# Hymba decoder step on one core: three prompt blocks go raw through the first projection, two of them side by side

## The chip, the core and the metric

The kernel runs on one NeuronCore of a Trainium2 chip. The metric is the device time of one execution in microseconds (us). Five engines work side by side, each with its own queue of instructions in program order: PE (TensorE, matmul), ACT (ScalarE), DVE (VectorE), POOL (GpSimd) and SP (SyncE, which in this kernel issues all DMAs before the change). "PEld" is PE's loading of stationary operands, which overlaps its matmuls.

## The reference

One layer of a decoder over 1024 prompt tokens and 32 sample tokens (8 sequences of 4), with D_MODEL 1024. Cut to what the change touches:

```python
h = rmsnorm(x, norm_w)                     # x * rsqrt(mean(x*x) + 1e-6) * norm_w, per token
proj = einsum('btd,dc->btc', h, w_in)      # 4104 columns, split among the heads
# hq, hf, hi (values of the HGRN heads), hgate | fq, fk, fv, ff, fgate
hg_v = hi                                  # 512 columns
y = x + w_out(concat[HGRN(hq, hf, hi) * silu(hgate), FoX(fq, fk, fv, ff) * silu(fgate)])
return rmsnorm(y, final_norm_w), new k, v, log-forget rows, recurrent states
```

A token's norm is one factor for the whole token. So the projection of x * norm_w without the factor, times the factor afterwards, gives the same row of values.

## The kernel before, in words

The prompt is cut into 8 blocks of 128 tokens, `tb` 0 to 7; the sample tokens are a ninth, `tb` 8 (`NB`). An input is kept as two halves of lower precision, `xhi` and `xlo`, and so is each weight (`hi`, `lo`); a product takes three matmuls (hi by hi, hi by lo, lo by hi). `Group.proj` (L357) does this for one block, for a range of the 8 slices `k` of D_MODEL, with the token block as the stationary operand and 512 weight columns streaming. A block of the first projection is 24 such matmuls into one PSUM bank; the pool `ps_pj` has two banks.

The order of every engine is the program order, written out by hand (`manual_schedule`). It has these stages:

- **Start** (L391 to L435). SP issues the loads of x (512 KB per block, `load_x`, L187) and of the weights `w_1` for the values (four pairs of slices, 512 KB each, `Group.load`). PE runs 14 matmuls on ones (`warm`, L228). Blocks 0 and 1 take a short path: ACT writes `xhi = x * norm_w` (`quick_hi`, L281), DVE writes `xlo` (`quick_lo`, L284), eight small instructions each; the token's factor comes from a square on ACT and eight one-column products on PE (`quick_sq`, `quick_r`), is kept in `rc`, and is applied by ACT when the bank is copied to `v` (L424, L435). ACT and DVE split the weights on the way (`Group.split`). PE does block 0 over all `k`, then block 1.
- **First projection** (L439 to L462), blocks 2 to 7, with the full norm. `norm_a` (L320) is a square on ACT (L243), a product with `norm_w` in place on POOL (L245) and a sum on DVE (L249). `norm_b` (L323) is one product with ones on PE, two ACT steps for the factor (L218, L219), two products on DVE (L265), two copies to `xhi` on ACT (L269) and two subtractions to `xlo` on DVE (L273). While block `tb` is on PE, `norm_b(tb + 1)` runs; `norm_a(tb + 2)` stands ahead of it. The weights `w_2` for the gates are loaded and split in between (L351, L354). ACT copies the bank to `v` at the end of a block (L462).
- **Gates** (L554 to L571). Eight groups, `gate_group` (L522), in the order tb = 2, 3, 4, 5, 6, 7, 0, 1: 48 matmuls in two halves of 260 columns, each half copied out by DVE (L526; L529 and L530). After each group comes a SiLU (`silu_mul`: ACT L379 to L381, DVE L382, ACT L383, POOL L384 and L386). Between group and SiLU stands one step of `again(0)` or `again(1)` (L298), the full norm of the two raw blocks, in three steps: the square, the POOL product and the DVE sum (L307); then the product with ones on PE, the factor, and the products (L313); then `xhi` and `xlo`. Groups 0 to 5 (by place) take one step each. Groups 3 to 5 also take a step of `lower_bound` (L511 on), groups 3 and 5 a split of the first slab (ACT L486, DVE L487).
- **The rest**: 24 slabs of 128 columns by all tokens, the HGRN recurrence, the FoX attention and the output projection, PE nearly always at work.

```python
anew = [again(0), again(1)]
for n, tb in enumerate((2, 3, 4, 5, 6, 7, 0, 1)):
    gate_group(tb)
    if n < 6:
        next(anew[n // 3])
    ...
    silu_mul(sg[tb // 2][:, tb % 2], 128)
```

Of the kernel before, what the change touches and what calls it, by code (L numbers as in the profile page):

```python
# [9 lines left out]
F32 = mybir.dt.float32  # L10
# [10 lines left out]
D = 1024  # L21
NB = 8
# [48 lines left out]
def tile_hymba(ctx, tc, x_prompt, x_sample, x_b, x_d, cache_k_t, cache_v, cache_logf_t, state_hgrn, page_table,  # L71
# [107 lines left out]
            debt[0] -= c  # L179
        debt[0] = max(debt[0], -3.0)  # L180

    A.preload_act_table_set("natural_log_exp_and_others")

    nwT = cst.tile([128, KB], F32, name="nwT")
    xts = {}

    def load_x(tb):  # L187
        n = 128 if tb < NB else ND
        xts[tb] = U((17, 18, 24, 25, 26, 27, 24, 25, 26)[tb], D, a=KB)[:, :, :n]
        SP.dma_start(xts[tb], (x_b[tb] if tb < NB else x_d).rearrange("p (k t) -> p k t", k=KB))  # L190

    cc = cst.tile([128, K_MK], F32, name="cc")
    ident = cc[:, K_ID:K_ID + 128]
# [34 lines left out]
    def warm(n):  # L228
        for _ in range(n):
            mm(pw[:, :128], ones, ones, True, True)  # L230

    warm(14)

    ss_ = {}

# [40 lines left out]

    rc = cst.tile([128, 2], F32, name="rc")

    def quick_hi(tb, k):  # L281
        A.activation(xhi[:, k, tb * 128:tb * 128 + 128], xts[tb][:, k], AF.Copy, scale=nwT[:, k:k + 1])
# [3 lines left out]
        V.scalar_tensor_tensor(xlo[:, k, t], xts[tb][:, k], nwT[:, k:k + 1], f32(xhi[:, k, t]),  # L286
                               op0=OP.mult, op1=OP.subtract)

    def quick_sq(tb):
        A.activation(U(15 + tb % 2, D, a=KB), xts[tb], AF.Square)  # L290

    def quick_r(tb):
        sq, p = U(15 + tb % 2, D, a=KB), ps_s()[:, :1]
        for k in range(KB):
            mm(p, sq[:, k], ones[:, :1], k == 0, k == KB - 1)
        rstd(rc[:, tb:tb + 1], p, D)

    def again(tb):  # L298

        xt, sq = xts[tb], U(7, D, a=KB)  # L300
        on, s, r = (U(6)[:, i * 128:i * 128 + 128] for i in range(3))
        if tb == 0:
            V.memset(on, 1.0)
        A.activation(sq, xt, AF.Square)
        for k in halves:
            G.tensor_mul(xt[:, k], xt[:, k], nwT[:, k, None].to_broadcast([128, 4, 128]))
        V.tensor_reduce(s, sq.rearrange("p k t -> p t k"), axis=AX.X, op=OP.add)  # L307
        yield
        p = ps_s()[:, :128]
        mm(p, on, s, True, True)  # L310
        rstd(r, p, D)
        for k in halves:
            V.tensor_mul(xt[:, k], xt[:, k], r[:, None, :].to_broadcast([128, 4, 128]))  # L313
        yield
        for f in (norm_hi, norm_lo):
            for k in halves:
                f(tb, k)
        yield

    def norm_a(tb):  # L320
# [67 lines left out]
    w1 = Group(w_1, range(8), (12, 13, 14, 28))  # L388
    w2 = Group(w_2, (8, 9, 10, 11, 28, 29, 4, 5), (13, 14, 12, 13))
    every = slice(0, 512)  # L390
    load_x(0)  # L391
    SP.dma_start(nwT, norm_w)
    w1.load(0)
    w1.load(1)
    load_x(1)
    w1.load(2)
    w1.load(3)
    load_x(2)
    load_x(3)
    ks = range(KB)  # L400
    for k in ks:
        quick_hi(0, k)
    for k in ks[:4]:
        quick_lo(0, k)
    w1.split(0, (V, V), (V, V))
    quick_sq(0)
    for k in ks[4:]:
        quick_lo(0, k)
    w1.split(1, (A, A), (V, V))
    load_x(4)  # L410
    load_x(5)
    SP.dma_start(cc, consts[:, :K_MK])
    pa, pb = ps_pj(), ps_pj()
    w1.proj(pa, 0, every, ks[:4])
    w1.split(2, (A, A), (V, V))
    w1.proj(pa, 0, every, ks[4:6])
    w1.split(3, (A, A), (V, V))
    quick_r(0)
    for k in ks:
        quick_hi(1, k)  # L420
    w1.proj(pa, 0, every, ks[6:])
    for k in ks:
        quick_lo(1, k)
    A.activation(v[0][:, 0], pa, AF.Copy, scale=rc[:, 0:1])  # L424
    w2.load(0)
    w2.load(1)
    red = norm_sq(2)
    quick_sq(1)
    red(0)
    w1.proj(pb, 1, every, ks)  # L430
    norm_b(2)
    quick_r(1)
    norm_a(3)
    load_x(6)
    A.activation(v[0][:, 1], pb, AF.Copy, scale=rc[:, 1:2])  # L435
    w2.load(2)
    SP.dma_start(bf, bcast_row(b_fox_f, FH))
    SP.dma_start(hw, bcast_row(hg_norm_w, HK))
    for tb in range(2, NB):  # L439
        if tb < 6:  # L440
            norm_a(tb + 2)
        if tb == 7:
            w1.proj_d(vd, every)
        ps = ps_pj()
        w1.proj(ps, tb, every, range(3))
        if tb == 6:
            norm_b(NB)
        if tb < 7:
            norm_b(tb + 1)
        if tb < 4:  # L450
            load_x(tb + 5)
        if tb == 5:
            norm_a(NB)
        w1.proj(ps, tb, every, range(3, 6))
        if tb < 5:
            w2.split(tb - 2)
        if tb == 3:
            w2.load(3)
        if tb == 7:
            w2.split(3)  # L460
        w1.proj(ps, tb, every, range(6, KB))
        A.activation(v[tb // 2][:, tb % 2], ps, AF.Copy)  # L462
# [87 lines left out]

    SP.dma_start(lb[:, 0], bass.AP(tensor=hg_lb.tensor, offset=hg_lb.offset, ap=[[1, 128], [128, NH]]))
    lbs = lower_bound()
    anew = [again(0), again(1)]
    for n, tb in enumerate((2, 3, 4, 5, 6, 7, 0, 1)):  # L554
        gate_group(tb)
        if n < 6:
            next(anew[n // 3])
        if n == NB - 1:
            log_sigmoid(lf.rearrange("p b h -> p (b h)"), zf.rearrange("p b h -> p (b h)"), 128, 64)
            V.tensor_copy(lfh, lf.rearrange("p b h -> p h b"))  # L560
            w2.proj_d(sgd[:, :260], slice(0, 260))
            w2.proj_d(sgd[:, 260:], slice(260, 520))
        if n in (3, 4, 5):
            next(lbs)
        silu_mul(sg[tb // 2][:, tb % 2], 128)
        if n == 0:
            slab_load(0)
        if n in (3, 5):
            slab_split(0, n // 5)
        if n == 5:  # L570
            slab_load(1)  # L571
# [986 lines left out]
```

## Time and profile before

| | |
|---|---|
| median of 3 runs | 778.69 us (778.48 to 779.23) |
| the profiled execution | 778.63 us, its span 776.8 us |
| mean granted TensorE clock | 0.985 |
| busy: PE, PEld, DVE, ACT, POOL | 744.2, 665.3, 466.2, 363.8, 314.5 us |
| DMA | 64.99 MB, mean 84 GB/s |

The span runs from the first to the last instruction; 1.8 us lie around it. "busy" counts an engine's own work, and two engines' busy times overlap. The granted clock of 1.00 is 2.4 GHz, 0.50 is 1.2 GHz.

### The profile page before, as it was taken

What the parts mean: (1) busy time and instruction counts of PE and PEld (TensorE: products, weight loads), DVE (VectorE), ACT (ScalarE), POOL (GpSimd) and SP (SyncE); (2) the same over time, 40 slices, a digit from 0 to 9 for tenths busy, and PEclk for the clock granted to TensorE, in tenths of its full rate; (3) what the DMA queues carried; (4) which work ended last, traced back from release to release, by engine and by line L of the source; (5) the groups of instructions that cost most, each with busy time, mean ns of one, the idle gap of its engine ahead of it and who ended that gap; (6) DMA issues with size and microseconds to landing.
All of it is one profiled execution on the core that took longest, in us unless ns stands there. A gap on an engine that the chain in (4) does not pass through costs nothing.

```text
span 776.8 us, 13010 instructions
## 1 busy us (share of the span) xinstructions
PE 744.2 (96%) x4835; PEld 665.3 (86%) x4835; DVE 466.2 (60%) x972; ACT 363.8 (47%) x853; POOL 314.5 (40%) x333
## 2 busy tenths in 40 slices
PE   8999989999999999998999999989999899999996
PEld 7778989998999999998998889979988786577886
DVE  5775454746647666267448854785478776667422
ACT  5663555434242432136547653757466521456322
POOL 0442545373371753635424553436344533232101
PEclk9999999999999999999999999999999999999999
DMA  8211000101221113003101011101111596713521
GB/s 332 97 35 40 1 19 12 60 7 55 82 83 58 55 32 109 28 31 117 51 29 57 30 57 53 57 30 55 55 57 57 182 334 207 266 62 119 202 81 55
DMA packets 27570, 64.99 MB, mean 84 GB/s; under 512 B 5395, under 2 KB 6547, under 8 KB 27507
## 3 DMA queue, kind: packets, MB, share of 16 engines
q1 hardware_dynamic: 27506, 64.16, 24.3%
q8 instruction: 38, 0.62, 0.3%
q14 instruction: 26, 0.21, 0.1%
HBM read 47.27 MB, written 16.88 MB: 83 GB/s over the span
## 4 chain that ended last, share of the span: by engine, by line
PE 74%; DVE 13%; ACT 8%; issue 3%; DMA 1%; POOL 1%; SPq 0%; DVEq 0%; ACTq 0%; POOLq 0%
PE pj L95 54%; PE ps L95 11%; PE po L95 3%; PE pt L966 2%; DVE u L897 2%; DVE u L971 2%; DVE st L936 1%; PE pt L95 1%; ACT u L970 1%; ACT u L946 1%; DMA u<-in_w_dram 1%; ACT xhi L269 1%; DVE u L832 1%; DVE u L853 1%; DVE u L998 1%
## 5 line engine op out<-in xcount | busy, mean ns | idle before, releaser
L95 PE MATMUL pj<-xhi,u 128*128 128x352 f32 x1152 | 316.1, 334 | 0.9 <-DVE u L487 0.5
L95 PEld LDWEIGHTS pj<-xhi,u 128*128 128x128 f32 x1152 | 207.6, 190 | 3.5 <-DVE u L487 0.8
L95 PE MATMUL pj<-xlo,u 128*128 128x352 f32 x576 | 187.1, 325 | 0.0
L95 PE MATMUL ps<-u,u 128*128 128x64 f32 (+6 forms) x984 | 133.3, 271 | 3.5 <-ACT u L946 2.6
L95 PEld LDWEIGHTS ps<-u,u 128*128 128x128 f32 (+2 forms) x984 | 115.6, 178 | 14.4 <-ACT u L946 4.4
L951 POOL TENSOR_SCALAR u<-u,st 128x128 f32<-128x128 f32 (+3 forms) x64 | 48.7, 761 | 154.2 <-DVE st L949 87.2
L95 PEld LDWEIGHTS pj<-xlo,u 128*128 128x128 f32 x576 | 109.7, 190 | 0.7
L95 PE MATMUL pj<-u,xhi 128*128 128x260 f32 (+1 forms) x384 | 91.9, 333 | 5.9 <-DVE u L526 3.4
L946 ACT ACTIVATE u<-ps,st 128x512 f32<-128x512 f32 (+2 forms) x96 | 55.1, 578 | 48.8 <-DVE st L939 21.4
L95 PEld LDWEIGHTS pj<-u,xhi 128*128 128x128 f32 x384 | 65.3, 195 | 14.1 <-DVE u L526 3.0
L696 POOL TENSOR_TENSOR u<-u,u 128x256 f32<-128x256 f32 (+1 forms) x56 | 41.9, 748 | 83.6 <-PE ps L95 78.1
L95 PE MATMUL pj<-h,u 128*128 128x512 f32 (+2 forms) x237 | 74.1, 384 | 0.5 <-DVE h L1087 0.5
L971 DVE TENSOR_TENSOR u<-pt,u 128x512 fp32r<-128x512 f32 (+1 forms) x80 | 48.5, 632 | 28.6 <-ACT u L970 28.0
L95 PE MATMUL pj<-u,xlo 128*128 128x260 f32 (+1 forms) x192 | 63.7, 332 | 0.0
L970 ACT ACTIVATE u<-pt 128x512 fp32r<-128x512 f32 (+1 forms) x80 | 41.9, 553 | 41.4 <-PE pt L966 33.8
L936 DVE TENSOR_REDUCE st<-ps 128x1 f32<-128x512 f32 (+2 forms) x96 | 53.4, 556 | 12.2 <-PE ps L95 9.6
L95 PE MATMUL po<-u,u 128*128 128x256 f32 (+1 forms) x320 | 52.0, 287 | 8.4 <-DVE u L971 4.5
L95 PEld LDWEIGHTS po<-u,u 128*128 128x128 f32 x320 | 44.3, 189 | 15.3 <-DVE u L971 7.5
L95 PEld LDWEIGHTS pj<-h,u 128*128 128x128 f32 (+1 forms) x237 | 42.4, 186 | 10.4 <-ACT u L852 1.2
L95 PE MATMUL pj<-u,u 128*128 128x512 f32 (+3 forms) x174 | 46.4, 435 | 2.7 <-ACT u L1254 2.1
L95 PE MATMUL pj<-w,u 128*128 128x512 f32 (+2 forms) x125 | 47.5, 380 | 0.0
L966 PE MATMUL pt<-cc,u 128*128 128x128 f32 x288 | 42.2, 274 | 0.6 <-ACT u L826 0.5
(252 smaller groups left out, 1149.5 us busy)
## 6 DMA issues: line engine op xcount, KB each, us to landing
u<-in_w_s_dram SPq DMA_DIRECT2D x24, 512.0 KB
out_dram<-u SPq DMA_DIRECT2D x12, 512.0 KB
u<-in_x_b_dram SPq DMA_DIRECT2D x8, 512.0 KB
u<-in_cache_k_t_dram SPq DMA_DIRECT2D x16, 256.0 KB
u<-in_cache_v_dram SPq DMA_DIRECT2D x16, 256.0 KB
m_s<-u SPq DMA_DIRECT2D x7, 512.0 KB
u<-m_s SPq DMA_DIRECT2D x14, 256.0 KB
w<-in_w_out_dram SPq DMA_DIRECT2D x12, 256.0 KB
```

What stands on the lines that cost most here:

```text
L95: PE.matmul(out, lhsT, rhs, start=start, stop=stop, skip_group_check=True)
L269: A.activation(xhi[:, k, t0:t0 + n], xt[:, k], AF.Copy)
L696: G.tensor_mul(k4[:, :, 0, :], k4[:, :, 0, :], f3[:, eb, 1:2].to_broadcast([128, n, m]))
L832: V.tensor_copy(hi, vo[:, :, 64 * i:64 * i + 64])
L853: V.scalar_tensor_tensor(t[:, s], gt[:, s], 0.0, t[:, s], op0=OP.min, op1=OP.subtract)
L897: V.tensor_sub(K2[o], kf[r, :T], f32(K1[r]))
L936: V.tensor_reduce(st[:, m:m + 1], ps, axis=AX.X, op=OP.min)
L946: A.activation(P[:, s], ps, AF.Exp, scale=-1.0, bias=st[:, lo:lo + 1], accum_out=st[:, 2 + m:3 + m])
L951: G.tensor_scalar(P[:, :e], P[:, :e], st[:, 4:5], 1.0, op0=OP.mult, op1=OP.mult)
L966: PE.transpose(p[:, c:c + 128], probs[n, b][:, j * 128:(j + 1) * 128], ident)
L970: A.activation(ph[:, :w], p[:, :w], AF.Copy)
L971: V.tensor_sub(pl[:, :w], p[:, :w], f32(ph[:, :w]))
```

## The change

It has four parts. The first loads are cut: the weights of the first pair in two halves, from ACT's queue, with `norm_w` between them; x of block 0 in two halves. Blocks 0 and 1 go side by side, slice by slice: for each `k` the three matmuls of block 0, then those of block 1. Block 2 also goes raw, and none of the three gets its factor at the copy to `v`; `quick_sq` and `quick_r` are gone. And `again` now runs for three blocks, two steps after each gate group, groups in the order 3, 4, 5, 6, 7, 0, 1, 2; its second step makes the factor also as a column (one more product on PE, two more ACT steps), and its third scales the block's rows of `v` on ACT. Blocks 6, 7 and the sample tokens load into other buffers, since block 2 stays in its own.

```diff
--- before.py
+++ after.py
@@ -179,15 +179,24 @@
             debt[0] -= c
         debt[0] = max(debt[0], -3.0)
 
-    A.preload_act_table_set("natural_log_exp_and_others")
-
     nwT = cst.tile([128, KB], F32, name="nwT")
     xts = {}
 
-    def load_x(tb):
+    def load_x(tb, parts=1):
         n = 128 if tb < NB else ND
-        xts[tb] = U((17, 18, 24, 25, 26, 27, 24, 25, 26)[tb], D, a=KB)[:, :, :n]
-        SP.dma_start(xts[tb], (x_b[tb] if tb < NB else x_d).rearrange("p (k t) -> p k t", k=KB))
+        xts[tb] = U((17, 18, 24, 25, 26, 27, 25, 26, 27)[tb], D, a=KB)[:, :, :n]
+        src = (x_b[tb] if tb < NB else x_d).rearrange("p (k t) -> p k t", k=KB)
+        for i in range(parts):
+            k = slice(KB // parts * i, KB // parts * (i + 1))
+            SP.dma_start(xts[tb][:, k], src[:, k])
+
+
+    raw1 = U(12, 1024, a=2)
+    A.dma_start(raw1[:, 0], w_1[0, :, :512])
+    A.dma_start(nwT, norm_w)
+    A.dma_start(raw1[:, 1], w_1[0, :, 512:])
+    load_x(0, 2)
+    A.preload_act_table_set("natural_log_exp_and_others")
 
     cc = cst.tile([128, K_MK], F32, name="cc")
     ident = cc[:, K_ID:K_ID + 128]
@@ -229,7 +238,7 @@
         for _ in range(n):
             mm(pw[:, :128], ones, ones, True, True)
 
-    warm(14)
+    warm(12)
 
     ss_ = {}
 
@@ -276,7 +285,7 @@
 
 
 
-    rc = cst.tile([128, 2], F32, name="rc")
+    rc = cst.tile([128, 3], F32, name="rc")
 
     def quick_hi(tb, k):
         A.activation(xhi[:, k, tb * 128:tb * 128 + 128], xts[tb][:, k], AF.Copy, scale=nwT[:, k:k + 1])
@@ -286,19 +295,10 @@
         V.scalar_tensor_tensor(xlo[:, k, t], xts[tb][:, k], nwT[:, k:k + 1], f32(xhi[:, k, t]),
                                op0=OP.mult, op1=OP.subtract)
 
-    def quick_sq(tb):
-        A.activation(U(15 + tb % 2, D, a=KB), xts[tb], AF.Square)
-
-    def quick_r(tb):
-        sq, p = U(15 + tb % 2, D, a=KB), ps_s()[:, :1]
-        for k in range(KB):
-            mm(p, sq[:, k], ones[:, :1], k == 0, k == KB - 1)
-        rstd(rc[:, tb:tb + 1], p, D)
-
     def again(tb):
 
         xt, sq = xts[tb], U(7, D, a=KB)
-        on, s, r = (U(6)[:, i * 128:i * 128 + 128] for i in range(3))
+        on, s, r = (U(6)[:, i * 128:i * 128 + 128] for i in (0, 2 * tb + 1, 2 * tb + 2))
         if tb == 0:
             V.memset(on, 1.0)
         A.activation(sq, xt, AF.Square)
@@ -306,15 +306,19 @@
             G.tensor_mul(xt[:, k], xt[:, k], nwT[:, k, None].to_broadcast([128, 4, 128]))
         V.tensor_reduce(s, sq.rearrange("p k t -> p t k"), axis=AX.X, op=OP.add)
         yield
-        p = ps_s()[:, :128]
-        mm(p, on, s, True, True)
-        rstd(r, p, D)
+        p = ps_s()[:, :129]
+        mm(p[:, :128], on, s, True, True)
+        mm(p[:, 128:], s, on[:, :1], True, True)
+        rstd(r, p[:, :128], D)
+        rstd(rc[:, tb:tb + 1], p[:, 128:], D)
         for k in halves:
             V.tensor_mul(xt[:, k], xt[:, k], r[:, None, :].to_broadcast([128, 4, 128]))
         yield
         for f in (norm_hi, norm_lo):
             for k in halves:
                 f(tb, k)
+        x = v[tb // 2][:, tb % 2]
+        A.activation(x, x, AF.Copy, scale=rc[:, tb:tb + 1])
         yield
 
     def norm_a(tb):
@@ -388,70 +392,54 @@
     w1 = Group(w_1, range(8), (12, 13, 14, 28))
     w2 = Group(w_2, (8, 9, 10, 11, 28, 29, 4, 5), (13, 14, 12, 13))
     every = slice(0, 512)
-    load_x(0)
-    SP.dma_start(nwT, norm_w)
-    w1.load(0)
+    w1.raw = {0: raw1}
+    load_x(1)
     w1.load(1)
-    load_x(1)
     w1.load(2)
     w1.load(3)
-    load_x(2)
-    load_x(3)
-    ks = range(KB)
-    for k in ks:
-        quick_hi(0, k)
-    for k in ks[:4]:
-        quick_lo(0, k)
-    w1.split(0, (V, V), (V, V))
-    quick_sq(0)
-    for k in ks[4:]:
-        quick_lo(0, k)
-    w1.split(1, (A, A), (V, V))
-    load_x(4)
-    load_x(5)
+    for tb in range(2, 6):
+        load_x(tb)
     SP.dma_start(cc, consts[:, :K_MK])
     pa, pb = ps_pj(), ps_pj()
-    w1.proj(pa, 0, every, ks[:4])
-    w1.split(2, (A, A), (V, V))
-    w1.proj(pa, 0, every, ks[4:6])
-    w1.split(3, (A, A), (V, V))
-    quick_r(0)
-    for k in ks:
-        quick_hi(1, k)
-    w1.proj(pa, 0, every, ks[6:])
-    for k in ks:
-        quick_lo(1, k)
-    A.activation(v[0][:, 0], pa, AF.Copy, scale=rc[:, 0:1])
+    for k in range(KB):
+        for tb in range(2):
+            if k % 4 == 0:
+                for i in range(k, k + 4):
+                    quick_hi(tb, i)
+                    quick_lo(tb, i)
+            if k % 2 == 0 and tb == 0:
+                w1.split(k // 2, (A, A), (V, V))
+        w1.proj(pa, 0, every, (k,))
+        w1.proj(pb, 1, every, (k,))
+    for k in range(KB):
+        quick_hi(2, k)
+        quick_lo(2, k)
+    A.activation(v[0][:, 0], pa, AF.Copy)
     w2.load(0)
     w2.load(1)
-    red = norm_sq(2)
-    quick_sq(1)
-    red(0)
-    w1.proj(pb, 1, every, ks)
-    norm_b(2)
-    quick_r(1)
     norm_a(3)
-    load_x(6)
-    A.activation(v[0][:, 1], pb, AF.Copy, scale=rc[:, 1:2])
+    A.activation(v[0][:, 1], pb, AF.Copy)
     w2.load(2)
     SP.dma_start(bf, bcast_row(b_fox_f, FH))
     SP.dma_start(hw, bcast_row(hg_norm_w, HK))
     for tb in range(2, NB):
-        if tb < 6:
+        if 2 < tb < 6:
             norm_a(tb + 2)
         if tb == 7:
             w1.proj_d(vd, every)
         ps = ps_pj()
-        w1.proj(ps, tb, every, range(3))
+        w1.proj(ps, tb, every, range(4 if tb == 2 else 3))
         if tb == 6:
             norm_b(NB)
         if tb < 7:
             norm_b(tb + 1)
-        if tb < 4:
-            load_x(tb + 5)
+        if tb == 2:
+            norm_a(4)
+        if tb < 5:
+            load_x(tb + 4)
         if tb == 5:
             norm_a(NB)
-        w1.proj(ps, tb, every, range(3, 6))
+        w1.proj(ps, tb, every, range(4 if tb == 2 else 3, 6))
         if tb < 5:
             w2.split(tb - 2)
         if tb == 3:
@@ -550,11 +538,11 @@
 
     SP.dma_start(lb[:, 0], bass.AP(tensor=hg_lb.tensor, offset=hg_lb.offset, ap=[[1, 128], [128, NH]]))
     lbs = lower_bound()
-    anew = [again(0), again(1)]
-    for n, tb in enumerate((2, 3, 4, 5, 6, 7, 0, 1)):
+    anew = [x for tb in range(3) for x in [again(tb)] * 3]
+    for n, tb in enumerate((3, 4, 5, 6, 7, 0, 1, 2)):
         gate_group(tb)
-        if n < 6:
-            next(anew[n // 3])
+        for x in anew[2 * n:2 * n + 2]:
+            next(x)
         if n == NB - 1:
             log_sigmoid(lf.rearrange("p b h -> p (b h)"), zf.rearrange("p b h -> p (b h)"), 128, 64)
             V.tensor_copy(lfh, lf.rearrange("p b h -> p h b"))
```

## Rows read from the trace of the kernel before

**Rows 1.** The page: the span, and the chain that ended last, by engine.

```profile
span 776.8 us, 13010 instructions
...
PE 74%; DVE 13%; ACT 8%; issue 3%; DMA 1%; POOL 1%; SPq 0%; DVEq 0%; ACTq 0%; POOLq 0%
```

**Rows 2.** The chain that ended last in order of time: start us, us, what.

```profile
16.96 7.05 PE pj L95 x30
...
100.78 7.55 PE pj L95 x48
```

**Rows 3.** The timeline, first loads: start us, us, engine line op out<-in count [idle before <-releaser].

```profile
1.67 0.91 SPq L343 DMA_DIRECT2D u<-in_w_dram  x2
...
4.43 2.45 ACT L282 ACTIVATE xhi<-u,nwT 128x128 fp32r<-128x128 f32 x8 [2.40 <-DMA nwT<-in_norm_w_dram]
...
7.92 0.43 DVE L353 CAST u<-u 128x512 fp32r<-128x512 f32 x1 [1.82 <-DMA u<-in_w_dram]
...
9.19 1.15 ACT L351 ACTIVATE u<-u 128x512 fp32r<-128x512 f32 x2 [1.37 <-DMA u<-in_w_dram]
```

**Rows 4.** Stretches: us, busy of PE, PEld, DVE, ACT, POOL, PEclk, DMA share, GB/s.

```profile
7.00:14.00 7.00, 5.34 (x14) 3.26 (x15) 5.99 (x13) 4.09 (x7) 0.00 (x0) 0.76 1.02 412
...
9.81:13.22 3.41, 3.40 (x8) 1.99 (x7) 3.38 (x9) 1.87 (x5) 0.00 (x0) 0.50 1.02 419
...
101.97:105.38 3.41, 3.41 (x18) 3.41 (x17) 1.87 (x7) 2.58 (x5) 0.70 (x1) 0.50 0.00 0
```

**Rows 5.** The timeline: the products of one column for the norm of block 0.

```profile
15.12 1.84 PE L95 MATMUL ps<-u,u 128*128 128x1 f32 x16
```

**Rows 6.** The timeline, 23 to 42 us: norm, evacuation and next norm of the first projection.

```profile
23.85 0.39 PE L95 MATMUL ps<-u 128*128 128x128 f32 x2
...
25.07 1.29 DVE L265 TENSOR_TENSOR u<-u,u 128x512 f32<-128x512 f32 x2 [1.61 <-ACT u L219]
...
35.25 0.58 ACT L462 ACTIVATE u<-pj 128x512 f32<-128x512 f32 x1
...
35.73 1.05 ACT L243 ACTIVATE u<-u 128x1024 f32<-128x1024 f32 x1
...
36.80 2.02 DVE L249 TENSOR_REDUCE u<-u 128x128 f32<-128x1024 f32 x1 [1.18 <-ACT u L243]
...
38.74 1.30 DVE L265 TENSOR_TENSOR u<-u,u 128x512 f32<-128x512 f32 x2
...
39.47 1.23 ACT L269 ACTIVATE xhi<-u 128x512 fp32r<-128x512 f32 x2 [2.04 <-DVE u L265]
...
40.61 1.15 ACT L351 ACTIVATE u<-u 128x520 fp32r<-128x520 f32 x2
...
41.67 0.58 ACT L462 ACTIVATE u<-pj 128x512 f32<-128x512 f32 x1
```

**Rows 7.** The timeline of the gate groups, 74 to 101 us.

```profile
74.62 0.17 DVE L529 TENSOR_TENSOR zf<-pj,bf 128x8 f32<-128x8 f32 x1 [2.00 <-issue]
...
75.17 1.92 DVE L307 TENSOR_REDUCE u<-u 128x128 f32<-128x1024 f32 x1
...
80.12 0.38 PE L95 MATMUL ps<-u 128*128 128x128 f32 x2
...
86.29 0.17 DVE L529 TENSOR_TENSOR zf<-pj,bf 128x8 f32<-128x8 f32 x1 [2.13 <-PE pj L95]
...
92.05 0.17 DVE L529 TENSOR_TENSOR zf<-pj,bf 128x8 f32<-128x8 f32 x1 [2.14 <-PE pj L95]
...
100.31 0.42 DVE L526 COPY u<-pj 128x260 f32<-128x260 f32 x1
```

**Rows 8.** Lines of the gate groups, 68.6 to 120 us: busy us, mean ns | idle before.

```profile
L383 ACT ACTIVATE u<-u 128x512 f32<-128x512 f32 x7 | 4.4, 633 | 5.4 <-DVE u L382 5.4
...
L382 DVE SCALAR_TENSOR_TENSOR u<-u,u 128x512 f32<-128x512 f32 x7 | 4.8, 691 | 6.2 <-ACT u L381 6.1
```

**Rows 9.** One line, the subtraction of a slab's split: duration ns min/median/max.

```profile
L487 DVE TENSOR_TENSOR u<-u,u x22: 669/706/1359, 99.0 to 321.5; 128x512 fp32r<-128x512 f32 x22
```

## The prediction

> **What bounds the kernel now.** I read the page first: the span is 776.8 us and 74% of the chain that ended last is PE [rows 1]. Whatever shifts PE's stream early in the kernel shifts the end by as much, as long as nothing downstream has slack, so I price the change as two shifts: of the start of the gate groups, and across them. The profiled execution took 778.63 us, 0.06 under the median; the sum is made against the former.
>
> In the timeline of the first loads, see how little PE has to do at first: x of block 0 and norm_w let ACT start at 4.43, the first weights are seen at 7.92, the second at 9.19 [rows 3]. Then the stretches: PE had work with gaps, and from 9.81 to 13.22 its granted clock was 0.50 (1.2 GHz) [rows 4]. At full clock 30 matmuls of the first projection take 7.05 us, 0.235 each [rows 2].
>
> From block 2 on, the projection isn't held by PE. From one copy of a bank (35.25) to the next (41.67) it takes 6.42 us, and the steps join end to end on ACT and DVE: square 35.73, sum 36.80, product 38.74, xhi 39.47, split of gate weights 40.61, copy [rows 6]. PE needs 24 × 0.235 = 5.64 of it.
>
> In the gate groups PE sets the pace, 5.76 us a group (86.29 to 92.05, the first small copy behind each group) [rows 7], but for one pause: DVE copies group 4's first half only at 100.31, group 5 begins at 100.78 and runs 7.55 us for 48 matmuls [rows 2, 7], part of it at clock 0.50 [rows 4].
>
> **The front: what it removes.** PE now needs block 1's x beside block 0's, so its arrival starts the stream. Transfers of 512 KB follow each other at 412 GB/s [rows 4], 1.27 us each. Early bound: x of block 0 was there by 4.43 [rows 3]; two more transfers give 7.0. Late bound: x of block 1 is now the third 512 KB in the order of loads, and the third of before was seen at 9.19. Two queues that start together take away at most the two issues that stood ahead of the first weights' (two issues take 0.91 [rows 3]); nothing shows that the slow stretch between 4.43 and 7.92 goes. I take 9.2 - 0.9 = 8.3.
>
> From there: 0.4 to the first xhi, 45 matmuls (48 less block 0's first three) at 0.235 are 10.6, and one stretch of 3.41 at 0.50 as before loses 1.7 [rows 4], since PE idles beforehand. Both blocks are done at 8.3 + 0.4 + 10.6 + 1.7 = 21.0. ACT and DVE keep ahead: a pair of slices costs PE 2.8, ACT 1.15 for the split [rows 6] plus the short path's eight small copies (2.45 per eight [rows 3]) per two pairs and blocks. The 3.7 us of the two groups of one-column products are gone (1.84 [rows 5], twice).
>
> Behind it: block 0's copy ends with block 1's matmuls; then, by rows 6, square of block 3 1.05, sum 2.02, product with ones to DVE product 1.22 plus the 0.06 to start it (4.35), 0.7 to xhi (5.05), xhi 1.23, square of block 4 (ends 7.25), its sum (9.3), the gate weights' subtraction 0.7, sum of block 5 (12.0), product 0.65, xhi 1.23, split 1.15, copy of block 3 at 14.85. That is 21.0 + 14.85 = 35.85, against 41.67: **5.8 us earlier**. Norm work, not PE, eats the rest of block 2's head start. From there the steps are those of before, and the lead is carried to the gates. With the bounds: 41.67 - (9.2 + 12.7 + 14.85) = 4.9 and, at 7.0 without the slow stretch, 41.67 - (7.0 + 11.0 + 14.85) = 8.8.
>
> Costed at nothing: three issues on ACT's queue ahead of its table load (some 1.3 us more, covered by the wait until 4.43; without it 1.3); two warm-up products fewer; the split of the first pair on ACT, covered by the wait for block 1; load_x of blocks 6, 7 and the sample tokens, which on SP now stand behind the gate weights and wait for the subtractions of blocks 3, 4, 5, three blocks ahead of their squares (uncovered: one transfer of 1.3).
>
> **The gates: what it adds.** Two steps of the repeated norm follow one group. Steps 1 and 2 of the same block meet behind groups 0 and 3. The sum of step 1 stands on DVE behind the group's last copies: 75.17 to 77.09 behind group 0, whose end is near 74.55 (copy L529 at 74.62). Step 2's product is next on PE; before, it stood one group later, at 80.12, and waited for nothing [rows 7]. Now PE waits 77.15 - 74.55 = 2.6, and group 1's matmuls, SiLU and all that follows queue behind it. The extra one-column product adds 0.2 (a sixteenth part of 1.84 is 0.115, two records [rows 5]). **Group 1 and 2 are 2.8 us late.**
>
> Behind group 2 come steps 2 and 3, then its SiLU, then step 1 of block 2. From group 2's end: 1.22 to the product, 0.65, xhi 1.23, scaling of the values 0.6 (like a copy of 512 columns, 0.58 [rows 6]), SiLU 3 × 0.63 + 0.69 + 0.63 [rows 8], square 1.05, sum 1.95, gaps 0.3: 10.2. Group 3's matmuls end at 6.25. **PE idles 3.95 us**, longer than behind group 0 because ACT is packed. From that product on, the chain of before follows: 1.22, products 1.3, lower bound 0.4, SiLU 3.2, ACT's split 0.6, DVE's 1.36 [rows 9], first copy 0.42, gaps 0.1: group 5 begins 8.6 later. Group 4, even at half clock, fits under it. So group 5 begins 18.8 after group 2's end; before, 100.78 - 86.25 = 14.5. That is 4.3 more. Group 5 then needs 5.75, not 7.55, because the slow stretch falls on group 4, which has cover: 1.8 back.
>
> Sum: 2.8 + 4.3 - 1.8 = 5.3. After PE's first pause the clock may fall and slow group 1 by up to 1.8 (group 5's loss before); between 7 and 14 PE was idle 1.66 us in all and such a stretch came with it [rows 4], so it is more likely than not, but only part may fall on group 1's matmuls: I take the half, 0.9. **The gates cost 6.2 us**; bounds 5.3 and 9.1 (clock in full, and 2.0 of the second rival). The scaling of block 0's and block 1's values and steps 3 lie under the groups.
>
> Together -5.8 + 6.2 = +0.4: 778.63 + 0.4 + 0.06 = **779.1 us**.
>
> **Rivals.** *First, the start is better than bounded by the row of before* (faster). If block 1's x is there at 7.0 and PE then keeps its clock, the front gains 8.8: 778.69 - 8.8 + 6.2 = 776.1. For it: two queues, halves that let ACT start earlier. Against: the weights alone came 3.5 us after x [rows 3], and no row says why.
>
> *Second, DVE and POOL hinder each other in the packed groups* (slower). The same subtraction took 0.67 to 1.36 us [rows 9], the long one while POOL worked for the SiLU. Six more DVE operations with two inputs stand in the two chains above beside POOL's; if three of them wait 0.67 each, the gates cost 2.0 more: 780.9. It decides from two waits on, given the forecast's 0.4. For it: the POOL product of step 1 and the SiLU's now fall together. Against: before, most such operations kept their short time.
> The Trainium skill (SBUF — State Buffer, Who interferes with whom) says that a DVE instruction with two inputs in SBUF contends with a POOL instruction that reads SBUF, and that the second to issue is fully blocked until the first ends. By it each of the six that meets a POOL operation waits up to the whole of it, and the sum would be 6.2 + 2.0 or more; the trace agrees in its one 1.36 against 0.67, but not as a rule for every meeting.
>
> **How the numbers follow.** 0.2% (1.6 us) is about what a measurement of this kernel can tell from no change. The forecast holds with 0.47 (777.1 to 780.3), the second rival or a late front with 0.29, the first rival with 0.24. All bounds together reach from 775.2 to 782.9; leaving one in ten on either side, 776.0 to 781.6.
>
> **What would show it.** Right: the copy of block 3 near 35.9; PE idle some 2.6 us behind group 0 and 4 us behind group 3, each with the product with ones waiting for DVE's sum; group 5 about 1.3 us later than in the kernel before (100.78 - 5.8 + 7.1 = 102.1), running 5.8 us. Wrong: block 1's first matmul well before 8.7; a front lead that isn't lost in the norms of blocks 3 and 4; a sum that ends before its group does; further pauses in slabs or attention that move the end apart from the gates.

## The result, and the profile after

The changed kernel takes 783.15 us (median of 4, 781.66 to 784.11), the kernel before beside it 778.59: ratio 1.0058, interval 1.0041 to 1.0075. It is 0.58% slower, and 1.6 above the top of the predicted range. The profiled execution took 781.66, 3.03 more than that of before, and is the fastest of the four. The page, to be set against [rows 1]:

```profile
span 779.9 us, 12970 instructions
...
PE 72%; DVE 15%; ACT 8%; issue 3%; DMA 1%; POOL 1%; ACTq 0%; DVEq 0%; POOLq 0%
```

PE's share of the chain is 2 points lower, DVE's 2 higher. The timeline of the start and the first projection (columns as in [rows 3]), to be set against [rows 3, 6]:

```profile
8.28 0.63 ACT L355 ACTIVATE u<-u 128x512 fp32r<-128x512 f32 x1 [1.36 <-DMA u<-in_w_dram]
...
8.82 1.26 ACT L291 ACTIVATE xhi<-u,nwT 128x128 fp32r<-128x128 f32 x4
...
9.26 0.73 PE L95 MATMUL pj<-u,xhi 128*128 128x512 f32 x2 [0.82 <-ACT xhi L291]
...
26.04 1.29 DVE L274 TENSOR_TENSOR u<-u,u 128x512 f32<-128x512 f32 x2 [1.38 <-ACT u L228]
...
32.76 2.48 POOL L254 TENSOR_TENSOR u<-u,nwT 128x512 f32<-128x512 f32 x2
...
33.48 2.31 DVE L274 TENSOR_TENSOR u<-u,u 128x512 f32<-128x512 f32 x2
...
35.83 0.63 ACT L278 ACTIVATE xhi<-u 128x512 fp32r<-128x512 f32 x1 [0.81 <-DVE u L274]
...
37.42 0.57 ACT L450 ACTIVATE u<-pj 128x512 f32<-128x512 f32 x1
```

Block 1's first matmul comes at 9.26, the copy of block 3 at 37.42: 4.25 ahead of before. The same two products of a norm take 1.29 at 26.04 and 2.31 at 33.48, where POOL multiplies the next block by the norm's weights. The lead reaches the gates whole: the first small copy, DVE's first operation behind a gate group, stands at 70.33 (74.62 before), 4.29 earlier.

What PE waited for between 60 and 125 us (the waits: us in total, times, longest; before, its only row was for L526, 3.4 in all, 2.8 of it ahead of group 5):

```profile
PE ps L95 <- DVE u L307: 7.8, 2, 5.3
PE pj L95 <- DVE u L514: 0.6, 1, 0.6
```

L307 is the sum of the repeated norm. The two pauses in the timeline of the gate groups, to be set against [rows 7]:

```profile
70.33 0.17 DVE L517 TENSOR_TENSOR zf<-pj,bf 128x8 f32<-128x8 f32 x1 [2.04 <-issue]
...
70.88 1.75 DVE L307 TENSOR_REDUCE u<-u 128x128 f32<-128x1024 f32 x1
72.68 0.61 PE L95 MATMUL ps<-u 128*128 128x128 f32 x4 [2.44 <-DVE u L307]
...
74.14 1.29 DVE L315 TENSOR_TENSOR u<-u,u 128x512 f32<-128x512 f32 x2 [1.51 <-ACT u L228]
...
79.21 0.17 DVE L517 TENSOR_TENSOR zf<-pj,bf 128x8 f32<-128x8 f32 x1 [1.87 <-PE pj L95]
...
79.62 2.78 DVE L282 TENSOR_TENSOR xlo<-u,xhi 128x512 fp32r<-128x512 f32 x2
...
80.36 2.94 POOL L306 TENSOR_TENSOR u<-u,nwT 128x512 f32<-128x512 f32 x2
...
84.78 0.50 PE L95 MATMUL ps<-u 128*128 128x128 f32 x4
...
85.66 1.29 POOL L388 TENSOR_TENSOR u<-u,u 128x512 f32<-128x512 f32 x1 [2.36 <-ACT u L387]
...
86.28 2.94 DVE L315 TENSOR_TENSOR u<-u,u 128x512 f32<-128x512 f32 x2 [0.63 <-ACT u L228]
...
87.03 1.64 POOL L390 TENSOR_TENSOR u<-u,hw 128x512 f32<-128x512 f32 x1
87.54 0.63 ACT L278 ACTIVATE xhi<-u 128x512 fp32r<-128x512 f32 x1 [0.97 <-DVE u L315]
...
89.26 0.63 ACT L278 ACTIVATE xhi<-u 128x512 fp32r<-128x512 f32 x1 [1.09 <-DVE u L315]
...
94.71 1.90 DVE L307 TENSOR_REDUCE u<-u 128x128 f32<-128x1024 f32 x1 [0.90 <-ACT u L304]
...
96.67 1.01 PE L95 MATMUL ps<-u 128*128 128x128 f32 x4 [5.32 <-DVE u L307]
...
105.21 0.42 DVE L514 COPY u<-pj 128x260 f32<-128x260 f32 x1
```

PE idles 2.44 behind group 0 and 5.32 behind group 3, each time until the product with ones has DVE's sum. The products L315, 1.29 behind group 0, take 2.94 behind group 2 beside two POOL products of a SiLU. The chain that ended last, to be set against [rows 2]:

```profile
97.68 8.02 PE pj L95 x48
105.77 6.02 PE pj L95 x48
```

These are groups 4 and 5. Group 4 runs slow (clock 0.50 from 95.5 to 102.3), but group 5 had to wait for DVE's copy at 105.21 anyway; so the slow stretch is covered. Group 5 needs 6.02, against 7.55 before. The last group's small copy comes 3.5 later than before and the span ends 3.1 later: nothing large happened behind the gates.

### The profile page after: what moved, and what is told of

Same layout as the page of the kernel before. It is cut to its first block, busy times and chain, and to the rows that moved or that the text cites. A ratio compares the mean times of both kernels' runs of the same rounds, so it can differ in the third digit from the quotient of the medians.

```text
span 779.9 us, 12970 instructions
## 1 busy us (share of the span) xinstructions
PE 740.3 (95%) x4805; PEld 659.9 (85%) x4805; DVE 470.6 (60%) x978; ACT 367.1 (47%) x866; POOL 316.5 (41%) x333
## 4 chain that ended last, share of the span: by engine, by line
PE 72%; DVE 15%; ACT 8%; issue 3%; DMA 1%; POOL 1%; ACTq 0%; DVEq 0%; POOLq 0%
PE pj L95 52%; PE ps L95 11%; PE po L95 3%; PE pt L954 3%; DVE u L885 2%; DVE u L959 2%; PE pt L95 1%; DVE st L924 1%; ACT u L934 1%; ACT u L958 1%; DMA u<-in_w_dram 1%; DVE u L820 1%; DVE u L307 1%; DVE u L841 1%; DVE u L821 1%
## 5 line engine op out<-in xcount | busy, mean ns | idle before, releaser
L95 PEld LDWEIGHTS pj<-xhi,u 128*128 128x128 f32 x1152 | 205.4, 188 | 3.5 <-DVE u L475 0.8
L95 PE MATMUL ps<-u,u 128*128 128x64 f32 (+7 forms) x952 | 129.7, 272 | 3.4 <-ACT u L934 2.5
L95 PEld LDWEIGHTS ps<-u,u 128*128 128x128 f32 (+2 forms) x952 | 111.9, 178 | 14.4 <-ACT u L934 4.4
L934 ACT ACTIVATE u<-ps,st 128x512 f32<-128x512 f32 (+2 forms) x96 | 55.1, 578 | 50.1 <-DVE st L927 21.7
L95 PEld LDWEIGHTS pj<-h,u 128*128 128x128 f32 (+1 forms) x237 | 42.4, 186 | 10.2 <-ACT u L840 1.0
```

The source lines that it names most:

```text
L95: PE.matmul(out, lhsT, rhs, start=start, stop=stop, skip_group_check=True)
L934: A.activation(P[:, s], ps, AF.Exp, scale=-1.0, bias=st[:, lo:lo + 1], accum_out=st[:, 2 + m:3 + m])
```

## The experiments

The theory is that the two packed pairs of steps (steps 1 and 2 of one block behind the same gate group) cost more than the front gains. Its rivals are the clock after the pauses, and a front held up by its loads or by DVE's order. Later one more was added: POOL stretches DVE's operations. Each kernel is the one after with the edit shown, unless said; "..." stands for lines that are left out. "a0", "a1", "a2" are the repeated norms of blocks 0 to 2. In the kernel after, their nine steps stand a0,a0 | a0,a1 | a1,a1 | a2,a2 | a2 behind groups 0 to 4; a bar divides the groups. Each ratio is to runs of the kernel before beside it, whose medians lie between 777.76 and 778.87.

| kernel | median us | ratio to before, interval |
|---|---|---|
| after | 783.15 | 1.0058, 1.0041 to 1.0075 |
| e2_before_packed | 784.08 | 1.0069, 1.0048 to 1.0090 |
| e1_spread | 777.96 | 0.9992, 0.9983 to 1.0001 |
| e11_first_apart | 779.89 | 1.0029, 1.0018 to 1.0040 |
| e3_filled | 782.34 | 1.0053, 1.0035 to 1.0072 |
| e4_sp_loads | 783.16 | 1.0060, 1.0044 to 1.0077 |
| e10_x1_first | 785.56 | 1.0096, 1.0080 to 1.0111 |
| e6_front | 782.81 | 1.0064, 1.0050 to 1.0078 |
| e7_no_pool | 783.95 | 1.0081, 1.0066 to 1.0097 |
| e12_no_silu_pool | 782.18 | 1.0047, 1.0034 to 1.0060 |
| e13_no_front_pool | 777.62 | 0.9991, 0.9980 to 1.0002 |
| e5_light | 772.79 | 0.9931, 0.9917 to 0.9944 |
| e8_before_light | 775.77 | 0.9977, 0.9965 to 0.9988 |
| e9_best | 773.33 | 0.9945, 0.9931 to 0.9958 |

Two things make single traces differ where the code does not. The start: with the front of after, the first small copy stands at 68.57 in e3_filled, whose clock was 1.00 from 7 to 20.6 us, and at 71.53 in e12_no_silu_pool, whose clock was 0.50 from 9.4 to 13.8. The end: from the last group's small copy to the end of the span the traces of these fifteen kernels take 653.6 to 657.8. So a place in the gates is compared from the first small copy on, and times by the ratios.

### The pauses

**Packing alone, on the kernel before.**

```diff
-        if n < 6:
-            next(anew[n // 3])
+        for i in {0: (0, 0), 1: (0,), 3: (1, 1), 4: (1,)}.get(n, ()):
+            next(anew[i])
```

> The kernel before with one edit alone: steps 1 and 2 of each repeated norm behind the same gate group (groups 0 and 3). No new work, the front untouched. Theory: PE pauses 2.5 us behind groups 0 and 3, the wait for group 4's copy stays, and the time rises by 4 to 6 us, to 782.5 to 785. Rival (packing alone is harmless, the pauses come with the third block): at most 1 us more than before.

It takes 784.08, by the ratio 5.4 more than before, with the front of before. Its waits of PE in the gates:

```profile
PE ps L95 <- DVE u L307: 4.8, 2, 2.4
PE pj L95 <- DVE u L526: 2.9, 2, 2.2
```

The packed pairs alone, with only two blocks and no other part of the change, cost more than the whole change did.

**Unpacking, on the kernel after.** No group has steps 1 and 2 of one block.

```diff
-    anew = [x for tb in range(3) for x in [again(tb)] * 3]
+    a0, a1, a2 = again(0), again(1), again(2)
+    anew = ((a0,), (a0, a1), (a0, a1), (a1, a2), (a2, a2))
...
-        for x in anew[2 * n:2 * n + 2]:
+        for x in anew[n] if n < 5 else ():
```

> The changed kernel with the nine steps of the repeated norms laid out so that no block's sum and the product that waits for it stand behind the same gate group (one step behind group 0, two behind groups 1 to 4). Same instructions, other order. Theory (two pauses of PE behind groups 0 and 3 ate the front's lead of 4.2 us): PE no longer waits for DVE's sum (7.8 us of it go), the groups cost about 2 us more than in the kernel before or less, and the time is 775.5 to 777.5. Rival (the third block's extra work on ACT, DVE and POOL is what costs, wherever it stands): other waits take the place of the two, and the time stays at 781 to 784.

777.96, 5.2 less than after: both waits for L307 are gone. One of 4.8 ahead of group 5 has come up in their place, as its rival had it in part, and keeps the kernel from more:

```profile
PE pj L95 <- DVE u L514: 5.4, 2, 4.8
```

**Only the first pair apart**, with the loop of e1_spread.

```diff
+    anew = ((a0,), (a0, a0, a1), (a1, a1), (a2, a2), (a2,))
```

> The kernel after with only the first of the two packed pairs taken apart: behind the groups stand a0 | a0,a0,a1 | a1,a1 | a2,a2 | a2 (each entry one step of the repeated norm of block 0, 1 or 2). The pause behind group 0 goes, the one behind group 3 stays as it is. Theory: the first pause costs 2.4 us, and up to 1.5 more in executions in which the clock falls after it, so 783.2 - 2.4 - 1 = 779.8 (779 to 781), and the pause behind group 3 keeps its 5.3 us. Rival: the three steps in one place behind group 1 delay group 2's copies instead and the time stays within 1 us of 783.2; or the second pause grows, because step 2 of block 1 now stands beside its step 3.

779.89. PE's waits in its gates:

```profile
PE ps L95 <- DVE u L307: 5.9, 2, 5.3
PE pj L95 <- DVE u L514: 0.9, 2, 0.6
```

The second pause is unchanged at 5.3, as the theory had it. By the ratios the gain is 2.3. In the traces, from the first small copy to the last, it is 1.5, though the pause was 2.4: with three steps behind group 1, DVE is late for group 2's copies, and the small copies of groups 1 and 2 are 7.6 apart (75.86 and 83.46; 5.96 in after).

### The clock

**PE kept busy through both pauses** by 9 and 20 matmuls whose result nobody reads, ahead of the product with ones.

```diff
+        q = ps_s()
+        for _ in range((9, 0, 20)[tb]):
+            mm(q, xhi[:, 0, 896:1024], w2.hi[0][:, every], True, True)
```

> The changed kernel with matmuls of no use in the two pauses (9 of 512 columns ahead of block 0's product with ones, 20 ahead of block 2's, 2.1 and 4.7 us at full clock). The pauses stay, but PE works in them. Theory (part of the loss, and the spread of the changed kernel's executions from 781.7 to 784.1, is the clock falling behind the pauses): median 780.5 to 782, executions within 1 us. Rival (the clock plays no part): 783 with the same spread.

782.34. No stretch at 0.50 before 358 us is left in its profile, yet the time is within 0.8 of after, and the intervals overlap. PE still waits 1.2 in all for L307, behind the added matmuls. A wait of 2.3 for DVE's first copy ahead of group 5 stands where group 4's slow stretch was: that stretch was covered. So the clock is not the main cost.

But the first pause is sometimes followed by a slow stretch without cover. The profiled execution of after had none; that of e4_sp_loads had. Its stretch behind the pause (columns as in [rows 4]) and its small copies of groups 0 and 1:

```profile
72.81:76.22 3.41, 3.41 (x18) 3.41 (x17) 1.96 (x3) 2.58 (x7) 0.00 (x0) 0.51 0.00 0
```

```profile
69.58 0.17 DVE L516 TENSOR_TENSOR zf<-pj,bf 128x8 f32<-128x8 f32 x1 [2.03 <-issue]
...
79.99 0.17 DVE L516 TENSOR_TENSOR zf<-pj,bf 128x8 f32<-128x8 f32 x1 [2.46 <-PE pj L95]
```

10.41 apart, against 8.88 in after: 1.5. Seven of the kernels here have this first pause without matmuls to fill it. In their traces the two copies are 8.88, 8.88 and 8.87 apart in after, e7_no_pool and e10_x1_first, whose clock stays at 1.00 there; 10.41, 10.40 and 10.37 in e4_sp_loads, e6_front and e13_no_front_pool; and 11.80 in e12_no_silu_pool, where the stretch at 0.50 is twice as long. The median of after is 1.5 above its profiled execution; the other three have no trace, so that this is the same 1.5 isn't shown.

### The front

**All first loads whole and from SP**, in the order of before.

```diff
-    A.dma_start(raw1[:, 0], w_1[0, :, :512])
-    A.dma_start(nwT, norm_w)
-    A.dma_start(raw1[:, 1], w_1[0, :, 512:])
-    load_x(0, 2)
+    load_x(0)
+    SP.dma_start(nwT, norm_w)
+    SP.dma_start(raw1, w_1[0].rearrange("p (a c) -> p a c", a=2))
```

> The changed kernel with the first loads whole and all from SP's queue (x of block 0, norm_w, first weights, x of block 1), the rest unchanged. Theory (the second queue and the halves bring at most the 0.9 us of two issues): block 1's first matmul 0.3 to 1 us later than the 9.26 us of the changed kernel, the time 0 to 1 us longer. Rival (the split loads carry the front's lead): first matmul of block 1 2 us or more later, the time 2 us or more longer.

783.16, no different from after. In its trace block 1's first matmul comes at 9.62, 0.36 later, as expected. So the second queue and the halves bring nothing that shows in the time.

**Block 1's copies ahead of the weights' split**, to see when its x lands.

```diff
-            if k % 2 == 0 and tb == 0:
-                w1.split(k // 2, (A, A), (V, V))
+        if k % 2 == 0:
+            w1.split(k // 2, (A, A), (V, V))
```

> The kernel after with the split of the first pair of weights moved on ACT and DVE behind the eight copies of block 1's first half, in place of ahead of them. It shows when x of block 1 has landed. Theory: x of block 1 is there some time before 8.28 us, where the second half of the first weights is seen, and its copies now stand before that; the start of PE's block 0 waits for the split instead, so PE's first projection matmul moves from 6.98 to about 9 and block 1's first one stays near 9.3 or later: no gain, 783.2 within 1 us. Rival, as predicted blind: x of block 1 itself is what is late; then its first copy stays at 8.3 or later and all of the first projection moves back by about 1 us, 784.

The timeline of its start:

```profile
8.67 1.28 ACT L291 ACTIVATE xhi<-u,nwT 128x128 fp32r<-128x128 f32 x4 [2.27 <-DMA u<-in_x_b_dram]
...
10.52 1.52 PE L95 MATMUL pj<-u,xhi 128*128 128x512 f32 x2 [4.27 <-ACT u L355]
```

x of block 1 itself is seen only at 8.67 (the prediction put it at 8.3): the rival holds. PE's first projection matmul, at 6.98 in after, moves to 10.52, and the time goes to 785.56, more than either side expected.

**Norm of the block after next behind the next one's**, for all blocks.

```diff
-        if 2 < tb < 6:
-            norm_a(tb + 2)
...
-        if tb == 2:
-            norm_a(4)
+        if tb < 6:
+            norm_a(tb + 2)
```

> The changed kernel with one edit in the first projection: the square and sum of block tb + 2 stand behind the norm of block tb + 1 for every block, not ahead of it (the change does so for block 2 alone). Theory (the front's lead is eaten by DVE's order, the sum of the block after next ahead of the product of the next block): the copy of block 3 moves from 37.4 to about 36, the blocks behind it take 5.9 instead of 6.4 us, the gates start 2 to 3.5 us earlier and the time falls by as much, to 779.5 to 781.5. Rival (PE or the loads set the pace there): 782.5 to 784.

782.81, no gain that shows. The copies to the values come at 29.22, 35.84 and 42.45: 6.6 a block, where 5.9 was expected, because PE now waits four times, 3.2 in all, for a block's sum. So this other order of DVE's work only moves the wait.

### DVE beside POOL

**The repeated norm without POOL**: its product with the norm's weights goes into eight small DVE operations.

```diff
-            G.tensor_mul(xt[:, k], xt[:, k], nwT[:, k, None].to_broadcast([128, 4, 128]))
...
-        for k in halves:
-            V.tensor_mul(xt[:, k], xt[:, k], r[:, None, :].to_broadcast([128, 4, 128]))
+        for k in range(KB):
+            V.scalar_tensor_tensor(xt[:, k], xt[:, k], nwT[:, k:k + 1], r, op0=OP.mult, op1=OP.mult)
```

> The changed kernel with POOL's product of the repeated norm (x by norm_w) taken off POOL: DVE's product does both factors, in eight small operations per block instead of two. Theory (DVE waits for POOL in the packed groups: the two products behind group 2 took 2.94 us, the two subtractions behind group 1 2.78, instead of 1.3 each): the subtractions fall to 1.3 to 1.5, the second pause from 5.3 to about 4.3, the time by about 1 us to 781.5 to 782.5. Rival (the pause is ACT's count of steps alone): subtractions and pause as they were, 783 or more.

783.95, a miss. The subtractions behind group 1 fall from 2.78 to 1.95, but the eight operations take longer than the two they replace, most of all beside the SiLU's POOL products, which were still there, and the longest wait for the sum is 5.6 (its timeline, behind groups 0 and 2):

```profile
73.49 2.19 DVE L313 SCALAR_TENSOR_TENSOR u<-u,nwT,u 128x128 f32<-128x128 f32 x8 [1.44 <-ACT u L228]
...
85.47 3.23 DVE L313 SCALAR_TENSOR_TENSOR u<-u,nwT,u 128x128 f32<-128x128 f32 x8 [0.59 <-ACT u L228]
```

**The one pair of SiLU products that lies beside L315 left out** (so one block of gates lacks its last factors).

```diff
-        silu_mul(sg[tb // 2][:, tb % 2], 128)
+        silu_mul(sg[tb // 2][:, tb % 2], 128, n != 1)
```

(with the argument false, `silu_mul` returns ahead of its two POOL products)

> The kernel after, in which POOL's two products of the SiLU of group 1 (by place, from 0) are left out, so that one block of gates lacks its last factors. Theory: the two DVE products of block 1's repeated norm, which took 2.94 us beside them, take 1.3; the pause behind group 3 falls from 5.3 to about 3.7, near the 3.95 forecast, and the whole comes out about 1.6 us earlier than the kernel after: 781.5 (780.9 to 782.3). Rival: the products stay long, or they shorten and the pause stays at 5 us because something else on ACT is late there; then 783 as before.

782.18, at the late end of what was expected. The time alone shows nothing: its six runs lie from 779.12 to 786.07, its interval overlaps that of after, and the profiled execution, the slowest of the six, lost 2.9 in group 1 to the clock. The place is as expected: L315 takes 1.29, and the longest wait for L307 falls from 5.3 to 3.7. From its timeline and its waits of PE in the gates:

```profile
90.25 1.29 DVE L315 TENSOR_TENSOR u<-u,u 128x512 f32<-128x512 f32 x2 [0.66 <-ACT u L228]
```

```profile
PE ps L95 <- DVE u L307: 6.2, 2, 3.7
```

**The pair in the first projection left out** (block 5's normed rows lack the weights).

```diff
-        for k in (slice(0, 4), slice(4, 8)):
+        for k in (slice(0, 4), slice(4, 8)) if tb != 5 else ():
```

> The kernel after, in which POOL's two products of block 5 with the norm's weights in the first projection are left out, so that this block's normed rows lack that factor. Theory: the two DVE products of block 4's norm beside them take 1.3 us in place of 2.31, the copy of block 3 to its values comes 0.9 earlier (36.5 in place of 37.4, with the same clock at the start), the gate groups start that much earlier, and the time falls by 0.9: 782.3 (781.6 to 782.8). Rival: PE catches up within the next blocks, which it isn't the bound of, so the gates start where they did and the time stays within 0.4 of 783.2.

Its timeline, for 33.48 and 37.42 of after:

```profile
32.78 1.28 DVE L274 TENSOR_TENSOR u<-u,u 128x512 f32<-128x512 f32 x2
...
35.70 0.58 ACT L450 ACTIVATE u<-pj 128x512 f32<-128x512 f32 x1
```

From product to copy 2.92 against 3.94, 1.0 less, and the gates keep it: both parts of the theory hold there. The median, 777.62, is far below what was expected, and the place doesn't account for it. In the traces the span is 2.8 shorter: 0.7 from an earlier start of that execution, 1.0 here, 1.0 lost in the gates to a slow stretch at 72.7, and 2.05 at once between 441 and 451 us, in the attention, whose code is the same. The timelines of DVE and POOL there, first after:

```profile
445.96 2.17 DVE L885 TENSOR_TENSOR u<-u,u 64x1024 fp32r<-64x1024 f32 x1
448.16 2.60 DVE L841 SCALAR_TENSOR_TENSOR u<-u,u 128x352 f32<-128x352 f32 x1
...
445.75 1.29 POOL L475 TENSOR_TENSOR u<-u,u 128x512 fp32r<-128x512 f32 x1
447.12 3.25 POOL L883 TENSOR_TENSOR u<-u,u 64x1024 fp32r<-64x1024 f32 x1
```

and e13_no_front_pool:

```profile
444.92 1.22 DVE L885 TENSOR_TENSOR u<-u,u 64x1024 fp32r<-64x1024 f32 x1
446.33 1.34 DVE L841 SCALAR_TENSOR_TENSOR u<-u,u 128x352 f32<-128x352 f32 x1 [0.19 <-ACT u L840]
...
445.00 2.29 POOL L475 TENSOR_TENSOR u<-u,u 128x512 fp32r<-128x512 f32 x1
447.37 2.55 POOL L883 TENSOR_TENSOR u<-u,u 64x1024 fp32r<-64x1024 f32 x1
```

Here DVE starts 0.08 ahead of POOL, and POOL's operation is the long one; in after POOL is 0.21 ahead, and DVE's is. The remaining 2.7 between the medians isn't in any trace, and stays open.

### Versions that are faster

**e1_spread with the lower bound and the first slab's split behind later groups**, against the wait ahead of group 5.

```diff
-        if n in (3, 4, 5):
+        if n > 4:
             next(lbs)
...
-        if n in (3, 5):
-            slab_split(0, n // 5)
-        if n == 5:
+        if n in (5, 6):
+            slab_split(0, n - 5)
+        if n == 6:
             slab_load(1)
```

> The kernel of e1_spread with the three steps of the lower bound moved from behind groups 3 to 5 to behind groups 5 to 7, and the two halves of the first slab's split from behind groups 3 and 5 to behind groups 5 and 6 (its next load with them). Theory (the pause of 4.8 us that e1_spread still has ahead of group 5 comes from these standing in one chain with the repeated norm's steps on ACT and DVE): the pause shrinks to under 1 us, the time is 772 to 775.5. Rival (the chain only moves): a pause of 3 us or more ahead of a later group, 777 to 779.

772.79: faster than both kernels. The longest wait falls from 4.8 to 2.1, where under 1 was expected. **The same edit alone on the kernel before**, without the change:

> The kernel before with only the second half of the edits of e5_light: the three lower-bound steps behind groups 5 to 7 (by place, from 0) in place of 3 to 5, and the two halves of the first slab's split behind groups 5 and 6. Theory: the kernel before has its own pause of 2.8 us ahead of group 5 and loses 1.8 there to the clock; both go, so 778.0 - 4.6 = 773.4, at least 774.5. Then the front of the change is worth nearly nothing of the 4.25 us of lead that its gate groups start with, since e5_light stands at 772.8 with that lead; three more steps of the repeated norm would have eaten it. Rival: the front's lead is kept where nothing pauses; then this kernel lies some 4 us behind e5_light, at 776.5 to 777.5, because the pause ahead of group 5 is partly refilled by the other steps behind groups 3 and 4.

775.77. By the ratios it is 0.46% (3.6 us) behind e5_light, so the rival's reading holds, though the time lies below the rival's range. The first small copies, here and in e5_light:

```profile
73.53 0.17 DVE L529 TENSOR_TENSOR zf<-pj,bf 128x8 f32<-128x8 f32 x1 [2.00 <-issue]
```

```profile
69.86 0.17 DVE L517 TENSOR_TENSOR zf<-pj,bf 128x8 f32<-128x8 f32 x1 [2.02 <-issue]
```

Its gate groups start 3.67 later, and its last group is still 3.4 behind; each kernel has one wait of some 2 us left in the gates (2.3 and 2.1). So the front's lead is real, and it lasts to the end where no packed pair pauses PE, even with a third repeated norm.

**e5_light with the edit of e6_front** brings nothing more:

> The edits of e5_light and e6_front together on the changed kernel. Theory (front and gates are two shifts that add): e5_light's time less 2 to 3.5 us, 769.5 to 773. Rival (an earlier start of the gates is given back there): within 1 us of e5_light.

773.33, with an interval that overlaps that of e5_light.

## Why the prediction was wrong

The outline held: a front lead of some us, and two pauses, behind groups 0 and 3, for the repeated norm's sum, that eat it. That the pauses come of the packing is shown from both sides: packing alone cost the kernel before 5.4, unpacking gave 5.2 back. The sizes of several terms did not hold, and the two largest errors went to one side. In the profiled execution:

| term of the sum | forecast | measured |
|---|---|---|
| front, copy of block 3 | -5.8 | -4.25 |
| end of group 0 to end of group 2 | +2.8 | +3.0 |
| clock in group 1 | +0.9 | 0 (1.5 in e4_sp_loads) |
| end of group 2 to start of group 5 | +4.3 | +6.3 |
| group 5 itself | -1.8 | -1.5 |
| sum | +0.4 | +3.55 |

The span is 3.1 longer, the rest is given back behind the gates. This accounts for the profiled execution, 2.6 over the forecast of 779.1; the median is 1.5 higher still, and that part has no trace.

- **x of block 1 seen at 8.3, both blocks done at 21.0.** In e10_x1_first it was 8.67; in after the split of the second half of the first weights stands ahead of it on ACT, and its first copy comes at 8.82. PE begins block 1 at 9.26 in place of 8.7 and is done at 21.7. The first rival (faster) falls here.
- **"Behind it [...] copy of block 3 at 14.85".** The chain behind it was right up to the product of block 4 (33.48 against 33.0, with 0.7 from the late start); there the products beside POOL's took 2.31 in place of 1.29. I had the row [rows 6] for an uncovered product and didn't ask what POOL does at that moment in the new order. e13_no_front_pool showed the 1.0.
- **"Group 1 and 2 are 2.8 us late"**: 3.0, measured from matmul to matmul (14.70 against 11.73 before).
- **"From group 2's end: [...] 10.2"**: 11.7 (84.94 to 96.67). The sum let xhi start 0.65 after the first product did and hid the second product under it; both products together took 2.94, so that the second xhi ended 4.95 behind group 2 in place of 3.1. The pause is 5.3 in place of 3.95. e12_no_silu_pool brought it to 3.7, so this is the second rival's mechanism: it costs 1.6 in this one place.
- **"8.6 later" to group 5**: 9.1. The product with ones ran at half clock (1.01, against 0.61 behind group 0).
- **"the half, 0.9", for the clock**: a mean of cases, none of which is 0.9. In the seven traces of the section on the clock, group 1 lost nothing three times, 1.5 three times and 2.9 once. Which of these an execution gets, no run shows.

So the step that failed is the pricing of DVE's two-input operations at their free length, 1.29 a pair, in the places where the change newly puts POOL work beside them: 1.0 in the front and 1.6 behind group 2. The sum was short by 3.15. To the 1.0 and 1.6 come 0.5 each for the late start and the chain from the product at half clock, 0.3 in group 5 and 0.2 in groups 1 and 2; the 0.9 for the clock, which was not lost in this execution, goes off (0.05 is rounding). I held the second rival at 2.0 in the gates alone (its time, by its own sum, is 781.1 and not 780.9) and gave it less weight than the forecast, because most such operations had kept their short time before. That was evidence on where they stood, not on what a meeting costs. In the kernel after, POOL's L388 ends at 86.95 and the first L315 0.6 later (87.54, when xhi starts), L390 ends at 88.67 and the second L315 0.55 later. The long one of [rows 9] had the same form already before the change:

```profile
112.37 1.29 POOL L384 TENSOR_TENSOR u<-u,u 128x512 f32<-128x512 f32 x1 [5.03 <-ACT u L383]
...
112.84 1.36 DVE L487 TENSOR_TENSOR u<-u,u 128x512 fp32r<-128x512 f32 x1 [1.22 <-ACT u L486]
```

L384 ends at 113.66, and L487 0.54 later. The Trainium skill (SBUF — State Buffer, Who interferes with whom) says of such a meeting that the second to issue is fully blocked. In these three the traces agree: POOL issued first, and DVE's operation ends nearly its own length behind POOL's end. The prediction's "but not as a rule for every meeting" was the wrong reading of them.

## What to carry to other kernels

Before an operation with two inputs on DVE goes on the critical path, look at what POOL does at that time in the new order; where a POOL product has started first, the price that fits here is the end of POOL's instruction plus nearly DVE's own length (0.55 to 0.6 of 0.65). Two dependent steps behind one piece of PE work make PE wait for the first step: 2.4 behind group 0 here, and 5.3 behind group 3, where ACT had more to do ahead of that step. An order in which steps 1 and 2 of a block never share a group turned 783.15 into 777.96, and moving the small work that was late next turned it into 772.79. Weigh the parts of a change apart: the front was worth some 3.6 us where no packed pair stood behind it (e5_light against e8_before_light), and the order of the steps, a free choice, cost more than that (5.2 by e1_spread).

## What had not been expected of the hardware

Which of DVE and POOL waits can hang on some tenths of a microsecond: at L885 and L475 the one that started first kept 1.22 or 1.29 and the other took 2.29 or 2.17. Around that swap the two traces drift 2.05 us apart, some 400 us behind the edit, in a stage that was not changed. And a pause of about 2.4 us on PE was followed by a stretch at 0.50 in four of seven profiled executions, that of e4_sp_loads among them, but not in that of the kernel after, whose pause was as long.
